# First projections of a decoder trunk: q, k, v and the gate block by block, weights on a second queue, products of constants first

## The chip, the cores and the metric

The kernel runs on one core of a Trainium2 chip. The metric is the device time of one execution in microseconds (us), the median of several runs. The profile shows one execution, instruction by instruction, on the engines TensorE (PE; its weight loads are PEld), VectorE (DVE), ScalarE (ACT), GpSimd (POOL) and SyncE (SP). DMA transfers are issued by an engine's instruction queue and carried by 16 DMA engines.

## What is computed

A trunk of two layers on one sequence of 512 tokens with 1024 features, all in float32. Layer 0 is forgetting attention with 16 heads of 64 features, layer 1 an HGRN2 recurrence; a gated MLP with a short causal convolution follows each, and a norm ends it. The change touches only the beginning of layer 0:

```python
h = rmsnorm(x, att_norm_g)
proj = h @ w_in                                   # [512, 3*1024 + 16]
q, k, v, fl = jnp.split(proj, [D, 2 * D, 3 * D], axis=-1)
logf = jax.nn.log_sigmoid(fl + b_f)               # one gate logit per head and token
c = jnp.cumsum(logf, axis=1)
logits = q k^T / 8 + (c[query] - c[key])          # causal
o = softmax(logits) @ v
x = x + o @ w_out
```

## The kernel before, in words

Features lie on the partitions, tokens on the free axis, so an operand of a projection is 8 blocks of 128 features by 512 tokens, and a PSUM bank holds 128 outputs by 512 tokens. Exactness of float32 comes from splitting each operand into two parts, high and low: `split` (lines 67 and 68) casts the high part on ScalarE and subtracts it on VectorE to have the low part. `mm3` (lines 82 to 84) then makes three products for each block of 128 features: high by high, high by low, low by high. A projection of 128 outputs is 8 blocks, so 24 products (`proj`); its weights come in one DMA of 512 KB (`chunk`, line 72, tile `raw_...`) on SyncE's queue, into a ring of two.

The norm's gain goes into the operand (`Norm.block`: xh on ScalarE, line 180, xl on VectorE), its row scale rstd into the product afterwards. The sum of squares is made by `Norm.square` (nacc, nsq) and summed over the partitions by a product with ones (`nss`, line 199), from which `rsqrt` takes rstd.

The start: SyncE issues the gains `gn`, the 8 blocks of x (`xin`) and the weights of the first q and k (`wst`, in pieces of 1, 3 and 4 blocks). As a block of x comes in, six products go into the banks `pj_q` and `pj_k` of heads 0 and 1. Then come `nss`, the projection v0 by `proj`, and the gate's projection with 16 columns (`pj_wf`, 24 products). GpSimd's queue loads the convolution's constants `cv`.

Everything after that in the attention layer follows an order written by hand: `conduct` lets `projections()` issue one block of a projection per step, for the pairs of heads 1 to 7 (q1, k1, v1, q2, ...), and puts side streams between the steps. `operands()` scales and splits q and k of a pair (`qk`: q32, qh, ql) and moves the parts by small DMAs on SyncE's queue into the operands KX, QX, KK and QQ (lines 333 to 341); `forget()` makes the cumulated gate from `pj_wf` as rows cc of KX; `values()` transposes v (`vT`, line 351). `maxima()` takes row maxima of the logits (products `mxp` of KX and QX, line 407, and a reduction with a mask on VectorE, line 409), `attend()` makes the transposed logits, exponentials and weighted values (pt, ph, pv). The framework's scheduler then keeps an order for each engine and adds the semaphores. DMA issues of SyncE and ScalarE take eight semaphores in turn; an issue waits until the eighth before it has landed.

Of the kernel before, what the change touches and what calls it, by code (L numbers as in the profile page):

```python
# [16 lines left out]
P = 128  # L17
D = 1024
# [10 lines left out]
# gain columns: att norm, hgrn norm, ffn norms, final norm, output norm, lower-bound logits  # L29
G_ATT, G_HGRN, G_FFN, G_FIN, G_ON, G_LB = 0, 1, 2, 4, 5, 6  # L30
# t-range starts of the transposed logits of key tile j
# [4 lines left out]
def trunk(ctx, tc, xT, gains, convs, bf, wqkv, wf, wo, wup, wdn, wh, wi, who, out):  # L36
# [8 lines left out]
    def bank(name):  # L45
        """a bank for a projection"""
        return ps.tile([P, S], F32, tag="b", name=name)

    def side(name):
        """a bank for what runs beside the projections"""  # L50
        return ps.tile([P, S], F32, tag="s", name=name)
# [26 lines left out]
    def flat(ap):  # L78
        return ap.rearrange("p a b -> p (a b)")
# [6 lines left out]
    def proj(ap, xh, xl, name, kb=NB, bank=bank):  # L86
        """[128 features, S tokens] = W^T x; one step is one block of rows of W"""
# [11 lines left out]
    def early(aps, xh, xl, name, *more):  # L99
        """projections begun while the last two blocks of operands are still to come: three, and one for each  # L100
        of more, a bank and when it is free, whose weights take the place of operands used up before"""
# [39 lines left out]
    def conduct(main, *sides):  # L141
        """main issues one block of rows of a projection per step; a side stream yields how many steps
        to leave to main, or what it waits for"""
# [26 lines left out]
    class Norm:  # L170
# [24 lines left out]
        def finish(self, load=True):  # L195
            """rstd of each token, on every partition"""
# [27 lines left out]
    # =============== layer 0: forgetting attention ===============  # L224
    oscope = ExitStack()
    opool = oscope.enter_context(tc.tile_pool(name="opool", bufs=1, side="right"))
    with tc.tile_pool(name="att", bufs=2, side="right") as ap_:
# [3 lines left out]
        A.preload_act_table_set("natural_log_exp_and_others")  # L231
        norm = Norm(G_ATT, "a")

        # first projections, block by block as x comes in
        xin = [opool.tile([P, S], F32, name=f"xin{j}", bufs=1, tag=f"oh{j}") for j in range(NB)]
        wst = [opool.tile([P, S], F32, name=f"wst{j}", bufs=1, tag=f"ol{j}") for j in range(6)]
        wqk = [[wpool.tile([P, 1024], F32R, tag=t, name=f"{t}_qk{w}") for t in ("wh", "wl")] for w in range(2)]
        pieces = ((0, 1), (1, 4), (4, 8))
        nc.sync.dma_start(gn, gains)
        nc.sync.dma_start(xin[0], xT[:, 0])  # L240
        for i, (a, b) in enumerate(pieces):
            for w in range(2):
                nc.sync.dma_start(wst[2 * i + w][:, :(b - a) * P], flat(wqkv[w * 8][:, a:b, :]))
            for j in range(max(a, 1), b):
                nc.sync.dma_start(xin[j], xT[:, j])
        oq, ok = bank("pj_q0"), bank("pj_k0")
        for j in range(NB):
            for i, (a, b) in enumerate(pieces):
                if j == a:
                    for w in range(2):  # L250
                        c = slice(a * P, b * P)
                        split(wqk[w][0][:, c], wqk[w][1][:, c], wst[2 * i + w][:, :(b - a) * P])
            norm.block(j, xin[j], sq=False)
            c = slice(j * P, (j + 1) * P)
            for o, (h, l) in zip((oq, ok), wqk):
                mm3(o, h[:, c], l[:, c], norm.xh[j], norm.xl[j], j == 0, j == NB - 1)
# [4 lines left out]
        fraw = opool.tile([P, NB, HEADS], F32, name="fraw", bufs=1, tag="ol6")  # L261
        nc.sync.dma_start(fraw, wf)
        fwh = opool.tile([P, NB, HEADS], F32R, name="fwh", bufs=1, tag="ol7")
# [616 lines left out]
```

## Time and profile before

| | us |
|---|---|
| median of 3 runs (1279.92 to 1281.11) | 1280.43 |
| span of the profiled execution | 1279.4 |
| TensorE busy | 1258.4 (98%) |
| VectorE busy | 803.0 (63%) |
| ScalarE busy | 589.8 (46%) |
| GpSimd busy | 40.4 (3%) |

The span runs from the first to the last recorded instruction of the profiled execution. TensorE is busy nearly the whole of it. A wait of TensorE is told in the timeline by a bracket behind the instruction: the idle time ahead of it, and the engine or DMA that ended it.

### The profile page before, as it was taken

The page shows a single profiled execution, that of the slowest core. Times are in us where ns is not written, and L with a number is a line of the kernel's source. Part 1 is how long each engine was busy: PE and PEld are TensorE (multiplying, and loading weights), DVE is VectorE, ACT ScalarE, POOL GpSimd, SP SyncE. Part 2 cuts the span into 40 slices and gives each one's busy share as a digit, 9 for nine tenths or more (in the row PEclk, how much of TensorE's full clock was granted, in tenths as well). Part 3 has the DMA queues.
Part 4 walks back from the last instruction along what each step waited for, and adds up shares of the span by engine and source line. Part 5 has one row for each costly group of instructions (what it writes and reads, how often), then busy time and mean ns, then how long its engine had stood idle before and what let it go on. Part 6 is the DMA issues. An engine that isn't in the chain of part 4 may idle for free.

```text
span 1279.4 us, 15645 instructions
## 1 busy us (share of the span) xinstructions
PE 1258.4 (98%) x5994; PEld 1042.7 (81%) x5994; DVE 803.0 (63%) x1235; ACT 589.8 (46%) x827; POOL 40.4 (3%) x110
## 2 busy tenths in 40 slices
PE   7999999999999999999999999999999999999997
PEld 5778888888888888888888888888888888888886
DVE  6767767387777777333367585566777777762233
ACT  6355556454444444222267565455544444442231
POOL 2011110000000000000100000000000000000001
PEclk9999999999999999999999999999999999999998
DMA  6544554233233333333322222222333333333321
GB/s 200 153 119 106 135 135 122 98 120 98 97 99 99 99 99 95 91 91 91 98 96 66 83 66 83 83 67 82 99 99 99 92 94 95 98 91 91 94 88 66
DMA packets 43306, 127.25 MB, mean 99 GB/s; under 512 B 5616, under 2 KB 8304, under 8 KB 43232
## 3 DMA queue, kind: packets, MB, share of 16 engines
q1 hardware_dynamic: 42592, 125.56, 32.6%
q8 instruction: 47, 0.77, 0.2%
q10 hardware_dynamic: 544, 0.52, 0.1%
q14 instruction: 27, 0.22, 0.1%
q0 software_dynamic: 96, 0.18, 0.1%
HBM read 111.43 MB, written 2.10 MB: 89 GB/s over the span
## 4 chain that ended last, share of the span: by engine, by line
PE 95%; DVE 2%; DMA 1%; ACT 1%; issue 0%; SPq 0%; POOL 0%; DVEq 0%; ACTq 0%
PE pj_up L82 12%; PE pj_up L84 12%; PE pj_up L83 12%; PE pj_dn L84 6%; PE pj_dn L82 6%; PE pj_dn L83 6%; PE i L629 1%; PE i L628 1%; PE i L626 1%; PE pj_who L83 1%; PE pj_wo L82 1%; PE pj_wo L83 1%; PE pj_who L84 1%; PE pj_who L82 1%; PE pj_wo L84 1%; PE pj_hf L82 1%
## 5 line engine op out<-in xcount | busy, mean ns | idle before, releaser
L84 PE MATMUL pj_up<-xh_f,wl_up 128*128 128x512 f32 x704 | 274.3, 390 | 0.0
L83 PE MATMUL pj_up<-xl_f,wh_up 128*128 128x512 f32 x704 | 274.3, 390 | 0.0
L82 PE MATMUL pj_up<-xh_f,wh_up 128*128 128x512 f32 x704 | 274.3, 390 | 0.0
L84 PEld LDWEIGHTS pj_up<-xh_f,wl_up 128*128 128x128 f32 x704 | 132.3, 188 | 27.5
L83 PEld LDWEIGHTS pj_up<-xl_f,wh_up 128*128 128x128 f32 x704 | 132.3, 188 | 27.3
L82 PEld LDWEIGHTS pj_up<-xh_f,wh_up 128*128 128x128 f32 x704 | 132.3, 188 | 27.2
L82 PE MATMUL pj_dn<-gh,wh_dn 128*128 128x512 f32 x330 | 131.0, 397 | 0.0
L84 PE MATMUL pj_dn<-gh,wl_dn 128*128 128x512 f32 x330 | 131.0, 397 | 0.0
L83 PE MATMUL pj_dn<-gl,wh_dn 128*128 128x512 f32 x330 | 131.0, 397 | 0.0
L67 ACT CAST wh_up<-raw_up 128x1024 fp32r<-128x1024 f32 x88 | 92.7, 1053 | 65.9 <-PE pj_up L83 51.5
L68 DVE TENSOR_TENSOR wl_up<-raw_up,wh_up 128x1024 fp32r<-128x1024 f32 x88 | 107.8, 1225 | 15.4 <-ACT wh_up L67 11.7
L68 DVE TENSOR_TENSOR wl_dn<-raw_dn,wh_dn 128x1024 fp32r<-128x1024 f32 (+1 forms) x45 | 51.1, 1136 | 97.9 <-ACT wh_dn L67 97.7
L543 DVE TENSOR_TENSOR us<-pj_up,rstd_f 128x512 f32<-128x512 f32 x88 | 60.6, 689 | 78.7 <-PE pj_up L84 78.6
L67 ACT CAST wh_dn<-raw_dn 128x1024 fp32r<-128x1024 f32 (+1 forms) x45 | 44.1, 980 | 140.4 <-PE pj_dn L83 114.0
L67 ACT CAST gh<-y 128x512 fp32r<-128x512 f32 x44 | 27.3, 620 | 115.5 <-DVE y L551 115.5
L546 ACT ACTIVATE y<-us,cv 128x512 f32<-128x512 f32 x88 | 71.7, 815 | 8.4 <-DVE us L543 7.3
L84 PEld LDWEIGHTS pj_dn<-gh,wl_dn 128*128 128x128 f32 x330 | 62.3, 189 | 15.0
L83 PEld LDWEIGHTS pj_dn<-gl,wh_dn 128*128 128x128 f32 x330 | 62.3, 189 | 15.0
L82 PEld LDWEIGHTS pj_dn<-gh,wh_dn 128*128 128x128 f32 x330 | 62.3, 189 | 15.0
L548 DVE SCALAR_TENSOR_TENSOR y<-us,cv,y 128x512 f32<-128x512 f32 x88 | 66.1, 752 | 3.0
L547 DVE SCALAR_TENSOR_TENSOR y<-us,cv,y 128x512 f32<-128x512 f32 x88 | 65.6, 745 | 0.2
L550 ACT ACTIVATE y<-y 128x512 f32<-128x512 f32 x44 | 27.8, 632 | 79.4 <-DVE y L548 79.4
(368 smaller groups left out, 2375.5 us busy)
## 6 DMA issues: line engine op xcount, KB each, us to landing
raw_up<-in_wup SPq DMA_DIRECT2D x88, 512.0 KB
raw_dn<-in_wdn SPq DMA_DIRECT2D x30, 512.0 KB
raw_dn<-in_wdn SPq DMA_DIRECT2D x15, 384.0 KB
raw_v<-in_wqkv SPq DMA_DIRECT2D x8, 512.0 KB
raw_wo<-in_wo SPq DMA_DIRECT2D x8, 512.0 KB
raw_hf<-in_wh SPq DMA_DIRECT2D x8, 512.0 KB
raw_hq<-in_wh SPq DMA_DIRECT2D x8, 512.0 KB
raw_hg<-in_wh SPq DMA_DIRECT2D x8, 512.0 KB
```

The source lines that it names most:

```text
L67: A.copy(dst_h, src)
L68: V.tensor_tensor(dst_l, src, dst_h.bitcast(F32), op=ALU.subtract)
L82: PE.matmul(o, wh_, xh_, start=first, stop=False)
L83: PE.matmul(o, wh_, xl_, start=False, stop=False)
L84: PE.matmul(o, wl_, xh_, start=False, stop=last)
L543: V.tensor_mul(u[:, 2:], o, rstd)
L546: A.activation(y, u[:, 2:], AF.Identity, scale=k(2), bias=k(3))
L547: V.scalar_tensor_tensor(y, u[:, 1:S + 1], k(1), y, op0=ALU.mult, op1=ALU.add)
L548: V.scalar_tensor_tensor(y, u[:, 0:S], k(0), y, op0=ALU.mult, op1=ALU.add)
L550: A.activation(ys[0], ys[0], AF.Silu)
L626: PE.matmul(o, xh[kk][:, ts_], hs, start=kk == 0 and i % 2 == 0, stop=False, skip_group_check=True)
L628: PE.matmul(o, xh[kk][:, ts_], ls, start=False, stop=False, skip_group_check=True)
```

## The change

- Eight products of two 128x128 tiles of ones (`warm`) stand first on TensorE; nothing reads their bank.
- The weights of the first q, k and v lie in a new input `wqkv0`, block by block: one DMA of 192 KB brings the three 128x128 blocks that go with one block of x. ScalarE's queue issues these, the gains and the gate's weights; SyncE's queue issues only the eight blocks of x. The table load on ScalarE now stands behind the issues.
- For each block of x: xh and xl, one split of 384 columns, nine products for q, k and v, and two for the gate. The gate's weights stand in `fw` with 48 columns, the high part in columns 0 to 15 and the low part from column 32 on, so that two products do what three did; the product of low weights and low x is thereby added. `forget()` adds the two groups of rows by a copy on ScalarE and an addition on VectorE.
- The squares are taken after all blocks; the projection of v0 by `proj` and the gate's 24 products behind it are gone.
- Comments and docstrings are gone.

```diff
+        warm = side("warm")
+        for i in range(8):
+            PE.matmul(warm[:, :P], ones, ones, start=True, stop=True)
...
-        nc.sync.dma_start(gn, gains)
-        nc.sync.dma_start(xin[0], xT[:, 0])
-        for i, (a, b) in enumerate(pieces):
-            for w in range(2):
-                nc.sync.dma_start(wst[2 * i + w][:, :(b - a) * P], flat(wqkv[w * 8][:, a:b, :]))
-            for j in range(max(a, 1), b):
-                nc.sync.dma_start(xin[j], xT[:, j])
-        oq, ok = bank("pj_q0"), bank("pj_k0")
+        nc.scalar.dma_start(gn, gains)
+        for j in range(NB):
+            nc.sync.dma_start(xin[j], xT[:, j])
+            nc.scalar.dma_start(wst[j], wqkv0[:, j])
+            if j == 0:
+                nc.scalar.dma_start(fraw, wf)
         A.preload_act_table_set("natural_log_exp_and_others")
+        fw = ap_.tile([P, NB, 48], F32R, name="fw", tag="tmp", bufs=3)
+        G.memset(fw.bitcast(F32), 0.0)
+        oq, ok, ov, of = bank("pj_q0"), bank("pj_k0"), lbank("pj_v0"), side("pj_wf")
         for j in range(NB):
...
             norm.block(j, xin[j], sq=False)
-            c = slice(j * P, (j + 1) * P)
-            for o, (h, l) in zip((oq, ok), wqk):
-                mm3(o, h[:, c], l[:, c], norm.xh[j], norm.xl[j], j == 0, j == NB - 1)
+            split(h[:, :3], l[:, :3], wst[j])
+            if j == 0:
+                split(fw[:, :, 0:HEADS], fw[:, :, 32:32 + HEADS], fraw)
+            for w, o in enumerate((oq, ok, ov)):
+                mm3(o, h[:, w], l[:, w], norm.xh[j], norm.xl[j], j == 0, j == NB - 1)
+            PE.matmul(of[:48], fw[:, j], norm.xh[j], start=j == 0, stop=False)
+            PE.matmul(of[:48], fw[:, j], norm.xl[j], start=False, stop=j == NB - 1)
         xh, xl = norm.xh, norm.xl
         for j in range(NB):
             norm.square(j, xin[j])
         rstd = norm.finish(load=None)
-        fraw = opool.tile([P, NB, HEADS], F32, name="fraw", bufs=1, tag="ol6")
-        nc.sync.dma_start(fraw, wf)
...
-        ov = finish(proj(wqkv[16], xh, xl, "v0", bank=lbank))
-        split(fwh, fwl, fraw)
-        of = side("pj_wf")
-        for k in range(NB):
-            mm3(of[:HEADS], fwh[:, k], fwl[:, k], xh[k], xl[k], k == 0, k == NB - 1)
...
-            V.tensor_mul(z, of[:HEADS], rstd[:HEADS])
+            A.copy(e, of[32:32 + HEADS])
+            V.tensor_tensor(z, of[:HEADS], e, op=ALU.add)
+            V.tensor_mul(z, z, rstd[:HEADS])
...
+        "wqkv0": np.stack([cols(w_in[:, :3 * D])[8 * w] for w in range(3)], axis=2),
```

The start of ScalarE's instructions, before. A bracket names what the instruction waits for; DMAHW0 to DMAHW7 are the DMAs' semaphores.

```order
L231 ACT_TABLE_LOAD
L180 ACTIVATE xh_a0_123<-xin0_84,gn_67 128x512 [waits DMAHW1_49,DMAHW0_49]
L67 CAST wh_qk0_98<-wst0_92 128x128 [waits DMAHW2_49]
L189 ACTIVATE nacc_a_211<-xin0_84 128x512
L67 CAST wh_qk1_100<-wst1_93 128x128 [waits DMAHW3_49]
```

And after the change, the same place of ScalarE:

```order
L242 DMA gn_67<-in_gains 128x64
L245 DMA wst0_100<-in_wqkv0 128x384
L247 DMA fraw_108<-in_wf 128x128
L245 DMA wst1_101<-in_wqkv0 128x384
L245 DMA wst2_102<-in_wqkv0 128x384
L245 DMA wst3_103<-in_wqkv0 128x384 [waits DMAHW1_49]
L245 DMA wst4_104<-in_wqkv0 128x384 [waits DMAHW3_49]
L245 DMA wst5_105<-in_wqkv0 128x384 [waits DMAHW5_49]
L245 DMA wst6_106<-in_wqkv0 128x384 [waits DMAHW6_49]
L245 DMA wst7_107<-in_wqkv0 128x384 [waits DMAHW0_49]
L248 ACT_TABLE_LOAD
L180 ACTIVATE xh_a0_136<-xin0_92,gn_67 128x512
```

Ten DMA issues now stand ahead of the table load and of xh of the first block, five of them with a wait on an earlier DMA.

SyncE's queue around the operands of the third pair of heads (KX0 gets the high part of k, kh_2), before:

```order
L72 DMA raw_q4_0_1228<-in_wqkv 128x1024
L333 DMA QX0_316<-qh_2_747 64x512
L334 DMA QQ0_318<-ql_2_748 64x512
L335 DMA QQ0_318<-qh_2_747 64x512
L333 DMA QX1_322<-qh_2_747 64x512
L334 DMA QQ1_324<-ql_2_748 64x512
L335 DMA QQ1_324<-qh_2_747 64x512
L338 DMA KX2_327<-cc_352 2x512
L72 DMA raw_k4_0_1280<-in_wqkv 128x1024
L339 DMA KX0_315<-kh_2_828 64x512
```

The same place after:

```order
L72 DMA raw_k4_0_1289<-in_wqkv 128x1024
L339 DMA KX2_334<-cc_359 2x512
L334 DMA QX0_323<-qh_2_756 64x512
L335 DMA QQ0_325<-ql_2_757 64x512
L336 DMA QQ0_325<-qh_2_756 64x512
L334 DMA QX1_329<-qh_2_756 64x512
L335 DMA QQ1_331<-ql_2_757 64x512
L336 DMA QQ1_331<-qh_2_756 64x512
L339 DMA KX3_340<-cc_359 2x512
L340 DMA KX0_322<-kh_2_837 64x512
```

The weights raw_k4 stood directly ahead of KX0's transfer and now stand nine places ahead of it. In the fourth pair it is the other way round: after the change raw_k5 stands directly ahead of the transfer of kh_3.

ScalarE's instructions around the cast kh_2 that this transfer carries, before (pt, ph: exponentials of the second pair; dn, o32: copies of its output pv):

```order
L67 CAST ph_1_c_809<-pt_1_c_805 128x512
L449 ACTIVATE pt_1_b0_850<-lg_1_b0_847 128x512
L67 CAST kh_2_828<-k32_2_826 128x512
L67 CAST ph_1_b0_853<-pt_1_b0_850 128x512
L449 ACTIVATE pt_1_b1_874<-lg_1_b1_869 128x512
L67 CAST ph_1_b1_878<-pt_1_b1_874 128x512
L474 COPY dn_1_757<-pv_1_0_843 64x512
```

The same place after:

```order
L450 ACTIVATE pt_1_b0_859<-lg_1_b0_856 128x512
L67 CAST ph_1_b0_862<-pt_1_b0_859 128x512
L450 ACTIVATE pt_1_b1_883<-lg_1_b1_878 128x512
L67 CAST ph_1_b1_887<-pt_1_b1_883 128x512
L475 COPY dn_1_766<-pv_1_0_852 64x512
L67 CAST kh_2_837<-k32_2_835 128x512
L476 COPY o32_1_767<-pv_1_0_852 64x512
```

The cast moved behind the pair's last exponentials and behind the copy dn of the pair's first output. On TensorE the transposes vT of v0 stood in the third block of the projection k1, 32 products after the start of q1; now they stand in the middle of v1, 60 products after it.

## Rows read from the trace of the kernel before

**Rows 1.** The page: its first line, and the chain's shares by engine.
```profile
span 1279.4 us, 15645 instructions
...
PE 95%; DVE 2%; DMA 1%; ACT 1%; issue 0%; SPq 0%; POOL 0%; DVEq 0%; ACTq 0%
```

**Rows 2.** Waits of TensorE, whole run: waiter <- releaser: us, count, mean us.
```profile
PE mxp L407 <- DMA KX<-kh: 2.0, 1, 2.0
...
PE mxp L407 <- DVE mx L409: 0.9, 4, 0.2
```

**Rows 3.** Timeline of TensorE, first 50 us: start, us, instruction, count [idle before <-releaser].
```profile
5.68 0.79 PE L82 MATMUL pj_q<-xh_a,wh_qk 128*128 128x512 f32 x1 [5.68 <-ACT wh_qk L67]
...
10.12 0.80 PE L82 MATMUL pj_q<-xh_a,wh_qk 128*128 128x512 f32 x1 [1.52 <-ACT xh_a L180]
...
13.26 0.39 PE L83 MATMUL pj_q<-xl_a,wh_qk 128*128 128x512 f32 x1
...
22.15 1.02 PE L199 MATMUL nss_a<-nacc_a,ones 128*128 128x512 f32 x2
...
33.09 0.39 PE L82 MATMUL pj_q<-xh_a,wh_q 128*128 128x512 f32 x1
...
38.53 0.39 PE L82 MATMUL pj_k<-xh_a,wh_k 128*128 128x512 f32 x1
...
41.28 0.63 PE L351 MATMUL vT<-ident,v 128*128 128x128 f32 x4 [0.78 <-DVE v L347]
...
43.83 0.74 PE L407 MATMUL mxp<-KX,QX 66*128 66x128 f32 x3
```

**Rows 4.** Timeline of ScalarE: its start, and a DMA issue of its queue.
```profile
0.80 1.28 ACT L231 ACT_TABLE_LOAD   x1 [0.80 <-PEq L868]
...
4.26 0.72 ACT L180 ACTIVATE xh_a<-xin,gn 128x512 fp32r<-128x512 f32 x1 [2.18 <-DMA xin<-in_xT]
...
7.32 0.51 ACT L67 CAST wh_qk<-wst 128x384 fp32r<-128x384 f32 x1 [0.56 <-DMA wst<-in_wqkv]
...
1266.09 0.42 ACTq L828 DMA_DIRECT2D out_y<-y  x1
```

**Rows 5.** Timeline of SyncE's queue: two DMA issues.
```profile
10.90 0.33 SPq L72 DMA_DIRECT2D raw_v<-in_wqkv  x1
...
41.18 0.49 SPq L339 DMA_DIRECT2D KX<-kh  x1
```

**Rows 6.** Windows: stretch, us, PE, PEld, DVE, ACT, POOL busy, PEclk, DMA share, GB/s.
```profile
0.00:9.00 9.00, 2.93 (x6) 1.82 (x6) 2.59 (x6) 3.95 (x7) 7.74 (x24) 1.00 0.68 195
9.00:10.00 1.00, 0.00 (x0) 0.00 (x0) 0.00 (x0) 0.65 (x2) 0.00 (x0) 1.00 1.01 375
...
11.00:12.00 1.00, 1.00 (x4) 0.81 (x3) 1.00 (x2) 1.00 (x3) 0.00 (x0) 1.00 1.05 406
...
84.00:89.00 5.00, 5.00 (x19) 4.19 (x19) 3.63 (x14) 2.11 (x3) 0.00 (x0) 0.66 0.11 22
```

**Rows 7.** Timeline around KX of the third and the fourth pair.
```profile
78.05 0.61 ACT L67 CAST kh<-k 128x512 fp32r<-128x512 f32 x1
78.09 0.33 SPq L72 DMA_DIRECT2D raw_k<-in_wqkv  x1
78.68 0.48 SPq L339 DMA_DIRECT2D KX<-kh  x1
...
83.02 0.50 PE L407 MATMUL mxp<-KX,QX 66*128 66x128 f32 x2 [1.99 <-DMA KX<-kh]
...
106.95 0.47 SPq L339 DMA_DIRECT2D KX<-kh  x1
...
110.79 0.42 PE L407 MATMUL mxp<-KX,QX 66*128 66x128 f32 x2
```

**Rows 8.** Timeline of VectorE: the gate's first step, v32, and a weight's low part.
```profile
33.34 0.67 DVE L306 TENSOR_TENSOR fz<-pj_wf,rstd_a 16x512 f32<-16x512 f32 x1
...
40.45 0.69 DVE L347 TENSOR_TENSOR v<-pj_v,rstd_a 128x512 f32<-128x512 f32 x1
...
42.25 1.21 DVE L68 TENSOR_TENSOR wl_k<-raw_k,wh_k 128x1024 fp32r<-128x1024 f32 x1
```

More of the change, by code (lines that the diff above doesn't have):

```diff
@@ L35, in trunk @@
 @with_exitstack
-def trunk(ctx, tc, xT, gains, convs, bf, wqkv, wf, wo, wup, wdn, wh, wi, who, out):
+def trunk(ctx, tc, xT, gains, convs, bf, wqkv, wqkv0, wf, wo, wup, wdn, wh, wi, who, out):
     nc = tc.nc
@@ L229, in tmp @@
             return ap_.tile([rows, S], F32, tag="tmp", name=name, bufs=3)
-        A.preload_act_table_set("natural_log_exp_and_others")
[L232 to L238, printed above, removed]
@@ L239, in trunk @@
-        nc.sync.dma_start(gn, gains)
-        nc.sync.dma_start(xin[0], xT[:, 0])
-        for i, (a, b) in enumerate(pieces):
-            for w in range(2):
-                nc.sync.dma_start(wst[2 * i + w][:, :(b - a) * P], flat(wqkv[w * 8][:, a:b, :]))
-            for j in range(max(a, 1), b):
-                nc.sync.dma_start(xin[j], xT[:, j])
-        oq, ok = bank("pj_q0"), bank("pj_k0")
-        for j in range(NB):
[L248 to L252, printed above, removed]
-            norm.block(j, xin[j], sq=False)
-            c = slice(j * P, (j + 1) * P)
-            for o, (h, l) in zip((oq, ok), wqk):
-                mm3(o, h[:, c], l[:, c], norm.xh[j], norm.xl[j], j == 0, j == NB - 1)
+        norm = Norm(G_ATT, "a")
@@ new lines, in trunk @@
+        warm = side("warm")
+        for i in range(8):
+            PE.matmul(warm[:, :P], ones, ones, start=True, stop=True)
+        xin = [opool.tile([P, S], F32, name=f"xin{j}", bufs=1, tag=f"oh{j}") for j in range(NB)]
+        wst = [opool.tile([P, 3, P], F32, name=f"wst{j}", bufs=1, tag=f"ol{j}") for j in range(NB)]
+        fraw = ap_.tile([P, NB, HEADS], F32, name="fraw", tag="tmp", bufs=3)
+        nc.scalar.dma_start(gn, gains)
[4 more added lines that the diff above has]
+                nc.scalar.dma_start(fraw, wf)
@@ new lines, in trunk @@
+        A.preload_act_table_set("natural_log_exp_and_others")
+        fw = ap_.tile([P, NB, 48], F32R, name="fw", tag="tmp", bufs=3)
+        G.memset(fw.bitcast(F32), 0.0)
+        oq, ok, ov, of = bank("pj_q0"), bank("pj_k0"), lbank("pj_v0"), side("pj_wf")
+        for j in range(NB):
+            if j % 2 == 0:
+                wh2, wl2 = (wpool.tile([P, 2, 4, P], F32R, tag=t, name=f"{t}_qkv{j}") for t in ("wh", "wl"))
+            h, l = wh2[:, j % 2], wl2[:, j % 2]
+            norm.block(j, xin[j], sq=False)
+            split(h[:, :3], l[:, :3], wst[j])
[5 more added lines that the diff above has]
+            PE.matmul(of[:48], fw[:, j], norm.xl[j], start=False, stop=j == NB - 1)
@@ L260, in trunk @@
         rstd = norm.finish(load=None)
-        fraw = opool.tile([P, NB, HEADS], F32, name="fraw", bufs=1, tag="ol6")
-        nc.sync.dma_start(fraw, wf)
-        fwh = opool.tile([P, NB, HEADS], F32R, name="fwh", bufs=1, tag="ol7")
-        fwl = ap_.tile([P, NB, HEADS], F32R, tag="tmp", name="fwl", bufs=3)
-        ov = finish(proj(wqkv[16], xh, xl, "v0", bank=lbank))
-        split(fwh, fwl, fraw)
-        of = side("pj_wf")
-        for k in range(NB):
-            mm3(of[:HEADS], fwh[:, k], fwl[:, k], xh[k], xl[k], k == 0, k == NB - 1)
         cv = cpool.tile([P, 2, 2 * NF, 4], F32, name="cv")
```

## The prediction

> **What bounds the kernel now.** I read the page first. The span is 1279.4 us, and in the chain of work that ended last TensorE has 95% [rows 1]; no other engine has more than 2%. So a change counts only where it takes TensorE's products away or moves a wait that stands ahead of one. The list of TensorE's waits, read next, names the two that lie near the change's reach: one of 2.0 us of the row maxima (mxp) for the transfer into KX, and four of 0.9 us together for the mask and maximum on VectorE (mx) [rows 2]. Then I read the start of the run, instruction by instruction, on TensorE, ScalarE and SyncE's queue, because the change rewrites it. TensorE's first product starts at 5.68, it waits 1.52 us for xh of the second block at 10.12, has an nss of 1.02 at 22.15, begins the projection q1 at 33.09, and waits 0.78 us for v at 41.28 [rows 3]. The start is set by ScalarE: activation table load from 0.80 to 2.08, first xh at 4.26 when x has arrived [rows 4]. From q1 on the two programs issue the same projections, so the moment at which q1 starts is what the new start has to be measured by, and after it what is late in the attention pairs.
>
> **The gain in products.** The gate's projection falls from 24 products to 16 (48 columns that hold both parts, in place of three products). The 24 products of q1, all at full clock, take 38.53 − 33.09 = 5.44 us, 0.227 each [rows 3]; 8 fewer are −1.8 us. The block stage is then 8 × 11 = 88 products, 88 × 0.227 = 20.0 us, where before 48 + 24 + 24 = 96 stood.
>
> **When the first product can start.** This is the largest term. Before, ScalarE issued no DMA at the start. Now its queue holds gn, eight weight blocks and the gate's weights, ahead of the table load and of the first xh. The DMAs take eight semaphores in turn, so a DMA issue waits until the eighth before it has landed; by the order of instructions the last weight issue waits for xin3, the fourth 256 KB block of x on SyncE's queue, which itself waits for gn. So ScalarE is held until xin3 has landed; then come one issue (0.42, a ScalarE issue of this kernel), the table load (1.28), xh (0.72) and the cast of 384 columns (0.51) [rows 4].
> Landing of xin3: in the first 9 us all queues moved 195 GB/s on average, 1.755 MB; after that 375 and 406 GB/s at an engine share of 1.01 and 1.05 [rows 6]. Some 0.18 MB of the 1.755 are the convolution's constants of GpSimd's queue. With the two queues taking even shares, x's first four blocks (1.05 MB) are there when some 2.28 MB have moved: 1.755 by 9.0, the rest at 375 to 400 GB/s, 10.35. If x gets 57% of the bytes (256 KB against 192 per block), it is 9.7. I take 10.0. Bounds: 6.9, when the queue of x gets everything until then (1.23 MB with the constants, 6.3 us at that mean, raised because the issue of xin3 itself waits for gn), and 11.2, from before's own queue: there the issue of the v weights at 10.90 waited for xin3 [rows 5], with 1.57 MB up to it; here xin3 and what ScalarE issues ahead of its first wait are 1.70 MB, 0.13 more at 390 GB/s, 0.3 us later.
> So the first xh starts at 10.0 + 0.42 + 1.28 = 11.7 (before 4.26) and the first product at 11.7 + 0.72 + 0.51 = 12.95 (before 5.68): 7.3 us later.
>
> **When q1 starts.** By then x and the weights of the later blocks are on the chip or nearly so, and a block of 11 products (2.5 us) hides the two casts of the next block (1.25 on ScalarE, and about as much on VectorE), so I take no waits between blocks. The clock: between 10.12 and 13.26 seven products took 3.14 us, 0.45 each, half speed after the idle start [rows 3]; I count the first seven as that, +1.5 us. The nss, whose squares now run after all blocks, costs 0.9 as before. Sum: 12.95 + 20.0 + 1.5 + 0.9 = 35.35, against 33.09: **+2.25 us**. Moving the landing between 6.9 and 11.2 moves this from −0.85 to +3.45. The late first product is mostly paid for by waits that go: before, between 5.68 and 33.09 there were 27.4 us for 97 products that need 22.7 (96 × 0.227 and 0.9).
> One rule speaks on the second queue. The Trainium skill, page "DMA: Bandwidth & Descriptors", section "Issuing engines are not separate DMA queues", says that transfers started by different engines end on the same 16 DMA engines and interleave, so that a second issuer only saves the issue time. By it the bytes come no sooner than above. The rows leave it open, since one queue moved 195 GB/s for 9 us and later 406; if the second queue filled the engines from the start, the sum would be that of the second rival.
>
> **The wait for v.** The gate's chain on VectorE runs from 33.34 (fz) to 41.14 (v32: 40.45 + 0.69) before, 7.8 us [rows 8]. After, it gets one ScalarE copy and one addition more (0.7 each by the 0.67 of fz), but vT stands after 60 products from q1's start, not after 32. Added up in the new order, the row scale (Ln, Exp and three steps of 0.69), q32, the low parts of two weights (1.21 each [rows 8]), the gate's steps with its scan, k32 and v32, v is ready 14.7 us after q1's start. TensorE gets there after 60 × 0.227 = 13.6: a wait of 1.1 in place of 0.78, **+0.3** (−0.8 to +1.2).
>
> **The wait for KX.** In before's third pair the k cast ends at 78.66; 512 KB of k weights had been issued at 78.09, directly ahead, and the KX transfers at 78.68 were used at 83.02, after a wait of 1.99: 4.34 us from issue [rows 7]. Where nothing large is ahead it was less: issue at 41.18, use at 43.83 without a wait, 2.65 us [rows 3, 5]. The order of SyncE's queue now has the same 512 KB nine transfers ahead of that KX, so I take this wait away: −2.0. With it goes the half clock that followed: 84 to 89 has a mean granted clock of 0.66 [rows 6], 5.0 × 0.34 = 1.7 us. Together **−3.7**. What covers it: the k cast now stands behind a copy that needs the first output of the pair before (pv_1_0), and from that to the maxima there are 19 products, 4.3 us; copy 0.58, cast 0.62 and 2.65 us make 3.85. The cover is 0.45 us thick. With 4.3 us in place of 2.65, the wait is 1.2, and the clock may fall again. In the fourth pair before had 106.95 to 110.79 without a wait, 3.84 us of slack [rows 7]; now 512 KB stand directly ahead and the slack is some 2.6 us.
> The attention operands are also packed closer after the change, where exponentials follow each other without a weight cast between: **+0.3** (0 to 1.0, from the 0.9 of four mx waits [rows 2]).
>
> **Sum.** +2.25 + 0.3 − 3.7 + 0.3 = −0.85 on the span of 1279.4, 1278.55. The runs' median, 1280.43, is 1.0 above the span, so **1279.6 us**. A measurement of this kernel tells 0.2%, 2.6 us, from no change; this is within it. The products saved do not appear as a gain because the start takes them.
>
> **Rivals.** (1) The second queue fills the DMA engines from the start. For it: shares of 0.68 in the first 9 us and 1.01 to 1.05 after [rows 6]; against it, the slow part may be the transfers themselves. At 400 GB/s from about 3.5 us on, xin3 lands at 7.4, 2.6 earlier: 1279.6 − 2.6 = 1277.0, and 1276.0 with the lower bound and no denser stretch. Faster. (2) Slower: KX's transfer ends last again, in the third pair or the fourth. It decides from 3.1 us between issue and landing in the third pair (2.65 + 0.45), from 2.6 in the fourth; before's two rows are 2.65 and 4.34. Then the −3.7 is not had, and the sum is +2.85: 1283.3; two such waits give 1285. For it: both slacks are thinner than before; against it: the large load is away from the third pair. (3) The change doesn't do what it says: the eight products of constants run at about 1 to 5 us, TensorE then idles some 8 us, and at the KX wait 1.99 us of idling was followed by the half clock. I count them at nothing; if the clock did stay up, −1.5, 1278.1; if the whole block stage waited block by block instead, +2.5, 1282.1.
>
> **How the numbers follow.** Forecast 0.50, with its own range 1277.7 to 1281.3 (landing 8.6 to 11.2, the other terms 0.5); 0.05 of it is under 1277.9. Rival 1: 0.20, faster. Rival 2: 0.20, nearly all of it slower (from 1283.0). Rival 3: 0.10, nearly all within 0.2%. Faster 0.25, same 0.55, slower 0.20. Range 1276.0 to 1283.6: it takes in rival 1 and the single wait of rival 2.
>
> **What would show it.** In the changed kernel's trace: the first xh at about 11.7, behind DMA issues and the table load on ScalarE; the first pj_q product at about 12.95, with half-speed products after it; 16 gate products; q1 at about 35.35; a wait of about 1.1 at vT; no wait of mxp for KX in the third pair, and no low clock after it. A first xh before 9, or a KX wait of over 1 us, makes the prediction wrong, each in its direction.

## The result

The changed kernel took 1286.66 us (median of 4 runs, 1286.00 to 1287.52), the kernel before 1280.77 (4 runs). The ratio is 1.0051, with a 95% interval from 1.0036 to 1.0065: 0.5% slower, by 5.9 us in the medians and by 5.5 in the profiled spans (1284.9 against 1279.4). The forecast was 1279.6 and no change, with a range up to 1283.6; the time lies outside it.

Where it went is soon told by three moments on TensorE: the start of the projection k1, the first product of the output projection wo, and the last product of the run. From the first wo product to the last one, both kernels take 1050.5 us (1050.54 and 1050.48), so nearly all of the difference lies ahead of it: k1 starts 2.84 us later (41.37 against 38.53), and from k1 to wo the attention stage takes 183.51 us against 181.15, 2.36 more. The first wo product, in the kernel before and in the changed kernel:

```profile
219.68 0.40 PE L82 MATMUL pj_wo<-oh,wh_wo 128*128 128x512 f32 x1
224.88 0.40 PE L82 MATMUL pj_wo<-oh,wh_wo 128*128 128x512 f32 x1
```

The list of TensorE's waits in the changed kernel (waiter <- releaser: us in total, times, longest):

```profile
PE pj_q L82 <- ACT wh_qkv L67: 7.4, 1, 7.4
PE mxp L408 <- DMA KX<-kh: 2.1, 2, 1.3
...
PE vT L352 <- DVE v L348: 0.9, 1, 0.9
PE lg_c L447 <- ACT pt_a L450: 0.8, 2, 0.5
...
PE rp L421 <- DVE rr L416: 0.4, 1, 0.4
PE pv L466 <- ACT ph_a L67: 0.3, 1, 0.3
```

The first row is the new start. Below it, KX still costs 2.1 us, about as much as the 2.0 of [rows 2], now in two waits in place of one, and there are waits for exponentials and their casts (lg_c, pv).

ScalarE's timeline of the changed kernel at the start (start, us, instruction, count):

```profile
0.81 0.41 ACTq L242 DMA_DIRECT2D gn<-in_gains  x1
...
2.22 7.65 ACTq L245 DMA_DIRECT2D wst<-in_wqkv  x7
9.90 1.28 ACT L248 ACT_TABLE_LOAD   x1 [9.90 <-DMA wst<-in_wqkv]
11.20 0.72 ACT L180 ACTIVATE xh_a<-xin,gn 128x512 fp32r<-128x512 f32 x1
```

ScalarE issues DMAs until 9.87, with seven issues of weights spread over 7.65 us by their waits, then loads the table, and makes the first xh at 11.20, where [rows 4] had it at 4.26. By the trace the last part of xin3 landed at 9.52 and the last of these issues began at 9.54, so ScalarE was held by what the prediction named. The first block of x and the gains had landed by 4.50.

TensorE's timeline of the changed kernel, at the start and at the two projections:

```profile
1.20 3.78 PE L236 MATMUL warm<-ones 128*128 128x128 f32 x16 [1.20 <-POOL ones L61]
12.37 0.80 PE L82 MATMUL pj_q<-xh_a,wh_qkv 128*128 128x512 f32 x1 [7.39 <-ACT wh_qkv L67]
...
17.23 0.60 PE L82 MATMUL pj_q<-xh_a,wh_qkv 128*128 128x512 f32 x1
17.66 0.40 PE L83 MATMUL pj_q<-xl_a,wh_qkv 128*128 128x512 f32 x1
...
35.50 0.80 PE L82 MATMUL pj_q<-xh_a,wh_q 128*128 128x512 f32 x1
...
41.37 0.39 PE L82 MATMUL pj_k<-xh_a,wh_k 128*128 128x512 f32 x1
```

The products of constants end at 4.98 (the trace counts two instructions for each of the eight), and 7.39 us of idling follow. The first twelve products stand some 0.43 apart (12.37 to 17.66), the next 0.23. After that no block waits for another up to nss, and q1 follows at 35.50. That first product of q1 takes 0.80 since it is recorded from a moment at which nss still runs; so k1, one projection later, is the better mark of the delay.

The KX transfers of the third and the fourth pair in the changed kernel. First ScalarE's timeline:

```profile
88.42 0.62 ACT L67 CAST ph_b<-pt_b 128x512 fp32r<-128x512 f32 x1 [0.66 <-POOL pt_b L452]
89.07 0.58 ACT L475 COPY dn<-pv 64x512 f32<-64x512 f32 x1
89.55 0.62 ACT L67 CAST kh<-k 128x512 fp32r<-128x512 f32 x1
...
113.65 0.62 ACT L67 CAST ph_b<-pt_b 128x512 fp32r<-128x512 f32 x1 [0.96 <-POOL pt_b L452]
114.17 0.61 ACT L67 CAST kh<-k 128x512 fp32r<-128x512 f32 x1
```

SyncE's queue in the changed kernel:

```profile
78.16 0.33 SPq L72 DMA_DIRECT2D raw_k<-in_wqkv  x1
...
90.20 0.46 SPq L340 DMA_DIRECT2D KX<-kh  x1
...
112.68 0.33 SPq L72 DMA_DIRECT2D raw_k<-in_wqkv  x1
114.82 0.47 SPq L340 DMA_DIRECT2D KX<-kh  x1
```

And TensorE's waits for them:

```profile
92.54 0.64 PE L408 MATMUL mxp<-KX,QX 66*128 66x128 f32 x3 [0.82 <-DMA KX<-kh]
...
117.13 0.50 PE L408 MATMUL mxp<-KX,QX 66*128 66x128 f32 x2 [1.29 <-DMA KX<-kh]
```

From issue to use it is 2.34 and 2.31 us here, against 4.34 in [rows 7]. The transfer has become fast, and the operand is late all the same: the k cast stands behind the cast of the last exponentials of the pair before, and this one waits for GpSimd's mask (0.66 and 0.96 us).

Windows of the changed kernel over these waits (columns as in [rows 6]):

```profile
91.00:96.00 5.00, 4.18 (x20) 2.92 (x19) 3.74 (x14) 0.84 (x2) 0.00 (x0) 1.00 0.81 184
115.00:120.00 5.00, 3.65 (x21) 3.01 (x20) 2.61 (x9) 2.30 (x5) 0.00 (x0) 1.00 0.80 207
```

The granted clock stays at 1.00 over these waits in this execution. The fall of [rows 6] is absent.

### The profile page after: what moved, and what is told of

It is laid out like the page before. It is cut to its first block, busy times and chain, and to the rows that moved or that the text cites. A ratio compares the mean times of both kernels' runs of the same rounds, so it can differ in the third digit from the quotient of the medians.

```text
span 1284.9 us, 15670 instructions
## 1 busy us (share of the span) xinstructions
PE 1259.9 (98%) x6002; PEld 1043.3 (81%) x6002; DVE 804.2 (63%) x1237; ACT 590.9 (46%) x829; POOL 39.2 (3%) x111
## 4 chain that ended last, share of the span: by engine, by line
PE 89%; issue 4%; ACT 3%; DVE 2%; DMA 1%; POOL 1%; DVEq 0%; ACTq 0%; POOLq 0%
PE pj_up L82 12%; PE pj_up L84 12%; PE pj_up L83 12%; PE pj_dn L82 6%; PE pj_dn L84 6%; PE pj_dn L83 6%; PE i L630 1%; PE i L629 1%; PE i L627 1%; PE pj_who L83 1%; PE pj_wo L82 1%; PE pj_wo L83 1%; PE pj_who L84 1%; PE pj_who L82 1%; PE pj_wo L84 1%
## 5 line engine op out<-in xcount | busy, mean ns | idle before, releaser
L68 DVE TENSOR_TENSOR wl_up<-raw_up,wh_up 128x1024 fp32r<-128x1024 f32 x88 | 107.8, 1225 | 15.4 <-ACT wh_up L67 11.7
```

The lines of the kernel that those rows point to most:

```text
L68: V.tensor_tensor(dst_l, src, dst_h.bitcast(F32), op=ALU.subtract)
```

## The experiments

All runs below are compared with runs of the kernel before on the same chip. The theory to be tested had two parts. The start: ScalarE is held by its own DMA issues, and TensorE pays for that with an idle stretch and slow products. The attention stage: its order of instructions has changed, and that order costs more than the one of before. The rivals: the bytes bound the start anyway; the stage is longer because nothing covers the row scale's chain any more; the KX transfers themselves are what is late.

### Start: the products of constants

```diff
-        for i in range(8):
-            PE.matmul(warm[:, :P], ones, ones, start=True, stop=True)
```

> The changed kernel without the eight products of constants. Theory (they are wasted: TensorE idles 7.4 us after them, and the first 12 real products run at half speed all the same): first product at 12.4, the same 12 products 0.43 apart, q1 as before, total within 0.5 us of the changed kernel (1286.7). Rival (they shorten the slow phase): more than 12 products at 0.43, total 1 us or more above 1286.7.

Measured: 1286.3 us, 1.0048 of before (1.0036 to 1.0061), the same as the changed kernel. TensorE's timeline without the constants:

```profile
12.44 0.79 PE L82 MATMUL pj_q<-xh_a,wh_qkv 128*128 128x512 f32 x1 [12.44 <-ACT wh_qkv L67]
...
15.17 0.63 PE L82 MATMUL pj_v<-xh_a,wh_qkv 128*128 128x512 f32 x1
15.59 0.47 PE L83 MATMUL pj_v<-xl_a,wh_qkv 128*128 128x512 f32 x1
15.91 0.40 PE L84 MATMUL pj_v<-xh_a,wl_qkv 128*128 128x512 f32 x1
```

The total is what the theory said, the number of slow products is not: here only seven are slow, and k1 starts at 40.54, 0.83 earlier than with the constants. That the constants lengthen the slow phase isn't shown by it: there is one profile of each. The Trainium skill, page "TensorE: Matmul & The Clock Gate", Part 1, says that the number of slow products at a start differs from run to run of one kernel. No kernel here has two profiles; e3 and e9 below, whose start has the same constants and loads as the changed kernel, have nine and twelve, which agrees with it. What is shown: eight constants that end 7.4 us ahead gain nothing.

```diff
-        for i in range(8):
+        for i in range(40):
             PE.matmul(warm[:, :P], ones, ones, start=True, stop=True)
```

> The changed kernel with 40 products of constants in place of 8, so that they reach to about 12 us and TensorE hardly idles ahead of the first real product. Theory (the changed kernel's start loses 2.4 us to twelve products at half speed after an idle of 7.4 us): the first products 0.23 apart, q1 at about 33.1, total about 1284.3. Rival (half speed has another cause than the idle): still about 12 products at 0.43, total 1286.7.

Measured: 1284.39 us, 1.0027 (1.0017 to 1.0037), 2.3 below the changed kernel in the medians, as expected; each of its runs (up to 1285.74) lies below each of the changed kernel's (from 1286.00). TensorE's timeline:

```profile
1.20 11.30 PE L236 MATMUL warm<-ones 128*128 128x128 f32 x80 [1.20 <-POOL ones L61]
12.63 0.50 PE L82 MATMUL pj_q<-xh_a,wh_qkv 128*128 128x512 f32 x1
...
13.82 0.39 PE L82 MATMUL pj_k<-xh_a,wh_qkv 128*128 128x512 f32 x1
14.05 0.40 PE L83 MATMUL pj_k<-xl_a,wh_qkv 128*128 128x512 f32 x1
```

The constants now reach to 12.50, and after three products that still wait for their operands the steps are 0.23 at once. k1 starts at 39.64, 1.73 earlier. So the slow products are here the price of the idling, and the constants help if little idling lies between them and the real work.

The granted clock tells what the slow products are in the profile of e9 below, whose constants end at 4.92 and whose twelve slow products run from 13.16 to 18.42. Windows of e9 (columns as in [rows 6]):

```profile
5.00:10.00 5.00, 0.00 (x0) 0.00 (x0) 0.00 (x0) 0.00 (x0) 3.76 (x11) 0.81 1.04 372
13.00:18.00 5.00, 4.84 (x11) 3.48 (x12) 5.00 (x10) 5.00 (x12) 0.00 (x0) 0.50 0.61 240
18.00:20.00 2.00, 2.00 (x9) 1.65 (x8) 2.00 (x5) 2.00 (x5) 0.00 (x0) 0.91 0.00 0
```

The clock is at half there (0.50, the lower of the two levels 1.2 and 2.4 GHz) from 8.1, when TensorE had idled since 4.92, to 18.4, where the steps become short. In the other profiles this column reads 1.00 over the start, also where the steps are 0.43.

### Start: the queue

```diff
-        nc.scalar.dma_start(gn, gains)
+        nc.sync.dma_start(gn, gains)
         for j in range(NB):
             nc.sync.dma_start(xin[j], xT[:, j])
-            nc.scalar.dma_start(wst[j], wqkv0[:, j])
+            nc.sync.dma_start(wst[j], wqkv0[:, j])
             if j == 0:
-                nc.scalar.dma_start(fraw, wf)
+                nc.sync.dma_start(fraw, wf)
```

> The changed kernel with gains, gate weights and the weight blocks issued by SyncE in the same order instead of ScalarE; nothing else changes, and the order of the attention stage stays. Theory (ScalarE is held by its own DMA issues until 9.9): first xh at about 4.3 in place of 11.2, first product at 5.6 to 6.5 in place of 12.4, no or short waits between blocks, q1 6 us earlier, total about 1280.5. Rival (the bytes bound the start: 3.7 MB for the eight blocks): TensorE waits from block to block, the last block's products end only 2 us earlier, total about 1284.5.

Measured: 1280.12 us, 0.9996 (0.9987 to 1.0005), 6.5 below the changed kernel, as the theory had it; the rival's 1284.5, by which the bytes bound the start, is refuted. ScalarE's timeline:

```profile
0.80 1.28 ACT L248 ACT_TABLE_LOAD   x1 [0.80 <-PEq L870]
4.60 0.72 ACT L180 ACTIVATE xh_a<-xin,gn 128x512 fp32r<-128x512 f32 x1 [2.51 <-DMA xin<-in_xT]
```

and TensorE's:

```profile
5.77 0.50 PE L82 MATMUL pj_q<-xh_a,wh_qkv 128*128 128x512 f32 x1 [0.79 <-ACT wh_qkv L67]
6.11 0.40 PE L82 MATMUL pj_k<-xh_a,wh_qkv 128*128 128x512 f32 x1
...
9.12 0.50 PE L82 MATMUL pj_q<-xh_a,wh_qkv 128*128 128x512 f32 x1 [1.00 <-ACT wh_qkv L67]
...
27.40 1.02 PE L199 MATMUL nss_a<-nacc_a,ones 128*128 128x512 f32 x2
27.85 0.80 PE L82 MATMUL pj_q<-xh_a,wh_q 128*128 128x512 f32 x1
```

The same bytes through one queue start the products 6.6 us earlier, at full speed from the second one, with one wait of 1.00 between blocks. q1 begins at 27.85, 5.2 us ahead of the kernel before. And yet the whole is no faster than before: the stage from k1 to wo takes 185.74 us, 4.6 more than before. What the start wins over the kernel before, the stage takes.

And e2 without the products of constants:

```diff
-        for i in range(8):
-            PE.matmul(warm[:, :P], ones, ones, start=True, stop=True)
```

> e2_all_on_sync without the eight products of constants. Theory (they pay where the real products follow within a microsecond: in e2 the first product at 5.77 ran at full speed): the first 8 products 0.43 apart, 1.6 us more there, of which the wait for the second block takes up to 1.0: q1 0.6 to 1.6 us later, total about 1281. Rival (they change nothing, as in e1): same as e2, 1280.1.

Measured: 1279.83 us, 0.9995 (0.9987 to 1.0004): in time the same as with them, so the rival holds for the time. In its profile ten products are slow and k1 starts at 34.64, 0.92 later than in e2, within what the theory gave; the stage was shorter by more than that (182.73, without a fall of the clock). Less than a microsecond can't be told in the total.

### Stage: is it the missing cover?

```diff
-            for w, o in enumerate((oq, ok, ov)):
+            for w, o in enumerate((oq, ok)):
                 mm3(o, h[:, w], l[:, w], norm.xh[j], norm.xl[j], j == 0, j == NB - 1)
...
         rstd = norm.finish(load=None)
+        for j in range(NB):
+            mm3(ov, *late[j], xh[j], xl[j], j == 0, j == NB - 1)
...
+        for j in range(NB):
+            PE.matmul(of[:48], fw[:, j], xh[j], start=j == 0, stop=False)
+            PE.matmul(of[:48], fw[:, j], xl[j], start=False, stop=j == NB - 1)
```

> The changed kernel with the products of v0 and of the gate behind nss, as in the kernel before, from the same weights and queues; 40 products thus stand between nss and q1 again and cover the row scale's chain. Theory (the attention stage loses about 2.5 us because nothing covers that chain any more and the stage's order is packed closer): q1 still starts at about 35.5, waits and short stalls between 33 and 135 us fall from 8.7 to about 5 us, total 1283 to 1284. Rival (the loss has nothing to do with the cover): stalls stay at 8 us or more, total 1286.5.

Measured: 1287.78 us, 1.006 (1.0047 to 1.0073). The expectation failed, and the time lies above the rival's 1286.5 too: the stage is not shorter but longer, 185.99 us, with a wait of 2.4 for KX and one of 2.3 for v. The cover by 40 products alone doesn't bring the old stage back.

### Stage: is it the order?

The kernel before, with the gate's edit alone (and the copy and addition in `forget()`):

```diff
-        split(fwh, fwl, fraw)
+        split(fw[:, :, 0:HEADS], fw[:, :, 32:32 + HEADS], fraw)
...
-            mm3(of[:HEADS], fwh[:, k], fwl[:, k], xh[k], xl[k], k == 0, k == NB - 1)
+            PE.matmul(of[:48], fw[:, k], xh[k], start=k == 0, stop=False)
+            PE.matmul(of[:48], fw[:, k], xl[k], start=False, stop=k == NB - 1)
```

> The kernel before with one edit of the change alone: the gate as 16 products with 48 columns, and the copy and addition in the gate's chain. Start and queues are those of before. Theory (8 products saved, 1.8 us, and the rest as before): 1279.0. Rival (any shift ahead of the attention stage lets the scheduler put it in another order, and that order decides): q1 starts 1.8 us earlier, but the k casts and KX come late elsewhere, total 1280.5 to 1282.

Measured: 1283.03 us, 1.002 (1.0011 to 1.0029). Eight products are saved, q1 starts at 30.79 in place of 33.09, and the kernel becomes 2.5 us slower. The theory failed; the rival has the direction, but the loss is larger than its 1282. By the names in the traces, 12 of ScalarE's 802 instructions from the row scale on (one is the copy that the edit adds) and 80 of TensorE's 5896 from q1 on stand elsewhere in the scheduler's order than before. One of the 12 is the k cast of the third pair. ScalarE's timeline of this run:

```profile
83.30 0.62 ACT L67 CAST ph_b<-pt_b 128x512 fp32r<-128x512 f32 x1 [0.66 <-POOL pt_b L454]
83.82 0.62 ACT L67 CAST kh<-k 128x512 fp32r<-128x512 f32 x1
```

TensorE's:

```profile
86.86 0.71 PE L410 MATMUL mxp<-KX,QX 66*128 66x128 f32 x3 [1.67 <-DMA KX<-kh]
87.37 0.63 PE L82 MATMUL pj_q<-xh_a,wh_q 128*128 128x512 f32 x1
87.80 0.63 PE L83 MATMUL pj_q<-xl_a,wh_q 128*128 128x512 f32 x1
```

and its windows:

```profile
87.00:91.00 4.00, 4.00 (x13) 3.02 (x14) 2.75 (x9) 0.00 (x0) 0.00 (x0) 0.57 0.90 215
```

The cast has moved behind the last ph_b, as in the changed kernel; KX is late by 1.67 us with no large transfer near (the last one was issued 4.6 us ahead), and the clock falls to half after it (steps of 0.43 at 87.37, granted clock 0.57). Two limits: the profile is of the fastest of the 11 runs (1281.41), and at the first wo product it shows 0.4 of the 2.5 us; and the edit also puts a copy and an addition into the gate's chain (the wait at vT is 1.1 in place of 0.78), so this run doesn't part the order from the longer chain.

The other way round: e2's start, arranged so that the order from q1 on is the old one. v0 and the gate, in 24 products as before, stand behind nss, and the squares are taken block by block.

```diff
-            norm.block(j, xin[j], sq=False)
+            norm.block(j, xin[j])
...
+        for j in range(NB):
+            mm3(ov, *late[j], xh[j], xl[j], j == 0, j == NB - 1)
...
+        for j in range(NB):
+            mm3(of[:HEADS], fwh[:, j], fwl[:, j], xh[j], xl[j], j == 0, j == NB - 1)
```

> The changed kernel with all loads issued by SyncE, the squares taken block by block, and v0 and the gate (24 products as in the kernel before) behind nss. The order of instructions from q1 on is then, but for a few rows, that of the kernel before. Theory (the attention stage's time hangs on that order): from the start of k1 to the first wo product 181 us as in before (after: 183.5), with before's KX wait of 2 us and its fall of the clock; q1 starts at 29.5 to 31, total 1277 to 1278.5. Rival (the stage loses because less stands ahead of it, whatever the order): 183 us or more, total 1280 or more.

Measured: 1278.93 us, 0.9989 (0.9981 to 0.9998). By the names in the traces TensorE's instructions from q1 on stand in the order of the kernel before, and ScalarE's too, but for one weight cast that comes earlier. k1 starts at 35.42, 1.7 later than in e2, and still this kernel is no slower: the stage takes 182.48, 3.3 less than in e2. Against the kernel before on the same chip it is 0.9989 where e2 has 0.9996, with intervals that overlap, so a gain over e2 is likely and not shown. It has the lowest median of the study, and is the only one whose interval lies below the kernel before, by little. Neither forecast came: the stage lies between the theory's 181 and the rival's 183, nearer the rival's, and the total 0.4 above the theory's 1278.5. Order alone therefore doesn't give the old stage back; here vT waits 1.0 us in place of 0.78 and two products of the maxima wait 0.7 together for ScalarE, which none did before, while KX costs 1.4 in place of 2.0.

The same with the gate as 16 products:

```diff
-            mm3(of[:HEADS], fwh[:, j], fwl[:, j], xh[j], xl[j], j == 0, j == NB - 1)
+            PE.matmul(of[:48], fw[:, j], xh[j], start=j == 0, stop=False)
+            PE.matmul(of[:48], fw[:, j], xl[j], start=False, stop=j == NB - 1)
```

> As e5_before_order with the gate as 16 products. Its order from q1 on is close to that of the kernel before, but not the same (the k cast of the third pair stands two places later on ScalarE). Theory (order decides): q1 1.8 us earlier than in e5, and the stage between 181 and 184 us, so a total from 1275.5 to 1279. Rival (8 products are 8 products): 1.8 us below e5.

From there on 8 of ScalarE's and 57 of TensorE's instructions stand elsewhere than in the kernel before. Measured: 1281.04 us, 0.9999 (0.9988 to 1.0009), 2.1 above e5 and outside both forecasts (theory up to 1279, rival 1277.1). q1 starts 1.27 earlier than in e5, and the stage takes 1.97 more, with one KX wait of 3.5 us. TensorE's wait, and the second of two DMA queues that were busy from 79 to 81 us:

```profile
82.47 0.50 PE L411 MATMUL mxp<-KX,QX 66*128 66x128 f32 x2 [3.47 <-DMA KX<-kh]
q8 instruction: 1, 0.02, 4.0%
```

Some 1.5 us of this wait is probably not the order's. By the landings in the trace 15 of the transfer's 16 parts had come by 80.92 and the last at 82.42, and one packet of 16 KB of the instruction queue had started at 79.92 and taken 1.27 us. Of the KX transfers up to 230 us in all profiles, four had a last part more than 0.6 us behind the others (this one, two in e3, one in before), and all four had such a packet in their course; that it held the part up is inferred from that. So the saving is lost again in the medians, but this profile doesn't show the order as its cause.

### KX: the cast or the transfer?

In the changed kernel:

```diff
-            split(th, tl, t32)
+            if w:
+                V.tensor_copy(th, t32)
+                V.tensor_tensor(tl, t32, th.bitcast(F32), op=ALU.subtract)
+            else:
+                split(th, tl, t32)
```

> The changed kernel with the high part of k cast by VectorE in place of ScalarE, so that it no longer stands behind the exponentials' casts there; the scheduler shifts some rows around it. Theory (KX comes late in the third and fourth pair since its cast waits in ScalarE's order, and the transfer itself takes only 2.3 us): the two KX waits of 0.8 and 1.3 us fall below 0.5 together, the other stalls of the stage stay at about 6 us; total 1284 to 1285.5. Rival (the transfer is what is late, behind 512 KB of weights): the KX waits stay at 2 us, total 1286.7.

Measured: 1287.38 us, 1.0055 (1.0043 to 1.0067). Half of the theory's waits: the one in the fourth pair is gone, the one in the third stays. The time is above both forecasts, nearer the rival's. The order shifted again, and in the third pair a weight load now stands directly ahead of KX, as it did before the change. SyncE's queue:

```profile
92.80 0.34 SPq L72 DMA_DIRECT2D raw_v<-in_wqkv  x1
93.24 0.47 SPq L344 DMA_DIRECT2D KX<-kh  x1
```

and TensorE's wait:

```profile
97.98 0.67 PE L412 MATMUL mxp<-KX,QX 66*128 66x128 f32 x3 [1.20 <-DMA KX<-kh]
```

That is 4.74 us from issue to use. Over the profiles, where TensorE waited: with 512 KB issued 0.4 to 0.6 us ahead of KX it was 4.34 (before), 4.37 (e3) and 4.74 (e9); 1.0 us ahead, 3.67 (e10); 1.85 us ahead, 2.51 (e5); 2.1 us ahead or farther, 2.31 and 2.34 (changed), 2.39 (e4). The nearer the load, the later the transfer, and beyond some 2 us no more. The one exception is e6 with 4.02 at 1.8 us ahead, which has the late part told above. In the traces the load itself lands 3.5 to 4.5 us after its issue, and where it was issued up to 1.0 us ahead KX landed 0.6 to 1.0 us after it. So both mechanisms appear in the rows, a late cast and a transfer behind a load, and the order decides which one strikes; no run moves the load alone.

The same edit in e5:

> e5_before_order with the same edit. There one KX wait of 1.4 us is left, followed by a fall of the clock that costs 1.7. Theory (late cast): the wait goes, and the fall with it; 2 to 3 us below e5, 1276 to 1277. Rival (the weights issued 1.9 us ahead make the transfer late, or the shifted rows cost what is saved): 1278.9 or more.

Measured: 1280.35 us, 1.0004 (0.9993 to 1.0016), its runs from 1278.22 to 1285.99. The KX wait of the third pair stayed (1.7 us, the load 1.0 us ahead). Nothing is gained, and the rival's number was nearer; the profile is of its fastest run (1278.22).

### The stage in all profiles

Times on TensorE, in us, from each kernel's one profile. A fall of the clock to half within the stage costs up to 1.7 us in [rows 6] (5.0 x 0.34) and in e4's windows above (4.00 x 0.43); the next to last column takes that off where a profile has one. A single profile can lie off its kernel's median (the profiled run by −2.1 us in e10, −1.6 in e4, +1.5 in e9, +1.2 in e2 and e3), so the last column gives the median of all runs less the start of k1.

| kernel | k1 starts | first wo product | stage | clock falls in it | stage less 1.7 | median less k1 |
|---|---|---|---|---|---|---|
| before | 38.53 | 219.68 | 181.15 | yes | 179.4 | 1242.2 |
| changed | 41.37 | 224.88 | 183.51 | no | 183.5 | 1245.3 |
| e1 | 40.54 | 224.65 | 184.11 | yes | 182.4 | 1245.8 |
| e2 | 33.72 | 219.46 | 185.74 | yes | 184.0 | 1246.4 |
| e3 | 41.27 | 227.26 | 185.99 | yes | 184.3 | 1246.5 |
| e4 | 36.23 | 220.07 | 183.84 | yes | 182.1 | 1246.8 |
| e5 | 35.42 | 217.90 | 182.48 | yes | 180.8 | 1243.5 |
| e6 | 34.12 | 218.56 | 184.45 | yes | 182.7 | 1246.9 |
| e7 | 34.64 | 217.36 | 182.73 | no | 182.7 | 1245.2 |
| e8 | 39.64 | 222.76 | 183.12 | no | 183.1 | 1244.8 |
| e9 | 42.13 | 227.21 | 185.08 | no | 185.1 | 1245.2 |
| e10 | 35.17 | 216.29 | 181.12 | no | 181.1 | 1245.2 |

The changed kernel, e1, e2, e7 and e8 have one and the same order from q1 on, and lie between 182.4 and 184.0 wherever their start is (k1 from 33.72 to 41.37). The kernel before and e5, with the old order, have 179.4 and 180.8. The medians part the two groups as well: 1244.8 to 1246.4 against 1242.2 and 1243.5. So the stage goes with the order, by some 1.3 to 1.6 us between the nearest of the two groups; but kernels of equal order differ by up to 1.6 too, and of the two with the old order the one that starts earlier has the longer stage. What the start adds is not parted from this.

## Why the prediction was wrong, step by step

**What bounds it.** Right: only TensorE's products and the waits ahead of them moved the time, and nothing after the attention stage changed.

**The first product.** Right, by its mechanism: 12.95 was forecast, 12.37 came; the first xh at 11.20 in place of 11.7, the landing of xin3 at 9.52 in place of 10.0. ScalarE was held as described, behind its own issues, until 9.87. The second queue brought a little: 246 to 259 GB/s over the first 9 us in the five profiles with two queues, 211 to 232 in the five where one queue has the same bytes, and 195 in [rows 6]. By the rule of the Trainium skill cited in the prediction, a second issuer saves issue time alone; the rows agree in that the share of the DMA engines from 9 to 12 us is 1.01 to 1.06 with two queues (the changed kernel) and 1.04 to 1.06 with one (e2). Rival 1 (xin3 at 7.4) is refuted; it is this rival, the first and not the second, that the prediction's sentence on a second queue means.

**The slow products.** Mis-sized: seven at half speed were counted, twelve came. From 12.37 to 17.66 is 5.29 us for twelve products that need 2.72 at 0.227, so 2.6 in place of 1.5. With the earlier first product this makes k1 2.84 late, where 2.25 was forecast for q1: 0.6 wrong. e8 shows the term: without the idling the kernel is 2.3 us faster.

**The waits between blocks, the gate, v.** Right: no waits between blocks, 16 products for the gate, and 0.9 us at vT where 1.1 was forecast.

**KX.** Wrong, in the step that says what covers it. The cover was measured from the end of the product pv_1_0 to the maxima, 4.3 us. But the copy and the k cast did not wait for pv_1_0, whose last product ended at 87.37: ahead of the copy dn on ScalarE stood the cast of the last exponentials of the pair before, which waited for GpSimd's mask, so the copy started 1.70 us later, at 89.07, and the cast at 89.55. The transfer took 2.3 us, even less than the 2.65 assumed, and TensorE waited 0.82 in the third pair and 1.29 in the fourth, about as much as in [rows 2] together: −2.0 was forecast, +0.1 came. The 1.29 is also the sign that the prediction itself named for being wrong (a KX wait of over 1 us). This is rival 2 by its place and by its direction, with another cause than the one named there. The other half of the term, the fall of the clock, did go in the profiled execution (1.7 us); but e1 and e2, with the same order, have it at 118 and 111 us, after the fourth pair's wait. Nor was it there to be had in most runs: no profile with such a fall has a mean granted clock above 0.997, and 45 of the 71 runs of the kernel before that stand beside the experiments have 0.998. Their medians in the three groups of runs are 1280.0 to 1280.5, what the kernel before takes anyway. The −1.7 was read from one profile and taken off a median that mostly holds no fall.

**The denser stage.** This is the step that failed most. 0.3 us (0 to 1.0) was written down for all exponentials and casts that now follow each other on ScalarE. By TensorE's timeline from k1 to 135 us, adding up every start of a product that came over 0.1 us later after its predecessor than such a product usually does, the changed kernel lost 8.3 us and the kernel before 4.6. KX makes 0.3 of the difference (2.44 against 2.16) and v 0.1; waits for exponentials, their casts and the row maxima (lg_c, pv, rp) make 3.3 us in the changed kernel, where before had one of 0.27; the rest are pieces of 0.1 to 0.3. So some 3.0 us came where 0.3 was forecast. The price was taken from the waits for mx, and these did not grow (0.6 in place of 0.9); what grew was of another kind, products that wait for ScalarE's exponentials and casts. In the profiles of e1, e2, e7 and e8, with the same order, the same waits return (lg_c for pt_a 0.8 us, rp 0.4, pv 0.3 and 0.2); in those of before and e5, with the old order, none of them stands.

**The sum.** 2.84 for the start, 0.1 for v, 0.3 − 1.7 for KX and the clock, 3.0 for the denser stage: +4.5 of the 5.15 us by which TensorE's last product is late in the one profile of each; 0.6 remains unassigned. The forecast had 2.25 + 0.3 − 3.7 + 0.3.

**The range.** It reached to one KX wait of rival 2 (1283.6); rival 2 with two waits was put at 1285 and left outside. What no case held was that the new order as a whole could be worse in many small places at once. The order of the rows stood there to be read before the run, and the prediction read it at two places only.

**Still open.** Why the scheduler's order changes as it does, and which of its moved rows costs what, was not tried one by one. The 182.4 to 184.0 us of equal orders shows that some 1.6 us of the stage depends on something else; that it is the moment at which things meet is not shown.

## What to carry to other kernels

A DMA issue in the queue of an engine that computes is an instruction of that engine: if it waits for an earlier DMA's semaphore, all that the engine has to compute waits behind it, so such issues belong on an idle engine's queue (e2; behind the first computation was not tried). Products of constants ahead of a late start paid here only where they reached to the first real product (e8); with ScalarE free they changed nothing measurable (e2 and e7). And where a scheduler orders a dense stage, a few products saved ahead of it can reorder it: compare the order of the dense stage before and after, row by row, before counting the saving, and measure an edit with the order kept as well.

## What was not expected of the hardware

- The clock column of the windows reads 1.00 over the start in every profile but e9's, also where products stand 0.43 us apart (12.37 to 17.66 of the changed kernel). In e9 it reads 0.50 over steps of the same length. So over the start the steps tell the speed, and a 1.00 in the column doesn't.
- After a gap of 0.79 to 1.57 us behind eight products of constants, the first real products ran at full speed (e2 from 5.77; e6, e5, e10); after 7.22 to 8.24 us (e3, the changed kernel, e9) they didn't.
- The same order of instructions had a fall of the clock in some profiles and none in others (e1 and e2 against the changed kernel, e7 and e8), with a loss of up to 1.7 us.
- A load of 512 KB issued up to 1 us ahead of a transfer of 128 KB on the same queue made it 3.7 to 4.7 us from issue to use, and from 2.1 us ahead on it took the 2.3 to 2.4 that it takes alone.
